# Loading the hi parts of streamed weights with a second, casting DMA on GpSimd's queue instead of copying them on ScalarE

## The chip, the cores and the metric

One NeuronCore of a Trainium2 chip runs the whole program. The metric is the device time of one execution in microseconds, lower is better. The kernel before was timed in three runs: 1090.1, 1091.72 and 1093.24 us, so the median is 1091.72 us.

## The reference

The reference is a two-layer decoder trunk in float32: 512 tokens, 1024 channels. Each layer normalises x (RMSNorm with a gain), multiplies it by a wide input projection, and feeds three mixers with slices of the result: a causal differential attention (4 heads of 2 x 64 dims, rotary), a gated convolution of width 3, and a chunkwise retention (4 heads). Each mixer's output is gated, projected to 1024 channels by its own matrix, weighted by a sigmoid gate, and the sum goes through an output projection back into x. A last RMSNorm closes it. Cut to what matters here:

```python
def hybrid_layer(x, norm_g, w_in, ..., w_branch, w_out, layer):
    h = rms_norm(x, norm_g)
    proj = h @ w_in
    (aq, ak, av, az, cx, cb, cc, cz, rq, rk, rv, rz, gates) = jnp.split(proj, split_points, axis=-1)
    a = diff_attention(aq, ak, av, ...) * silu(az)
    c = short_conv(cx, cb, cc, conv_w) * silu(cz)
    r = retention(rq, rk, rv) * silu(rz)
    merged = sum(sigmoid(gates[i]) * (branch[i] @ w_branch[i]) for i in range(3))
    return x + merged @ w_out
```

## The kernel before, in words

**Products in parts.** TensorE multiplies in the type fp32r, which keeps fewer bits than float32. So every float32 operand is split into a hi part (the value rounded to fp32r) and a lo part (the value minus its hi part), and `mm3` (L186 to L189) adds three products: hi by hi (L187), hi of the weight by lo of the activation (L188), lo of the weight by hi of the activation (L189). The split of a tile is a copy by ScalarE that rounds (L183) and a subtraction (L180), done by VectorE or GpSimd.

**The weight stream.** The weights of both layers are laid out as 184 chunks of 128 partitions x 1024 float32 (512 KB), in the order of use (`chunk_order`). A chunk feeds 24 products of TensorE (8 blocks of K, three products each). `prefetch` (L196) issues the load of a chunk into a buffer `wraw` on SyncE's queue; there are three such buffers. `split_next` (L203) takes the oldest loaded chunk and makes its parts `whi` and `wlo`, three buffers each. It works on two halves of 512 columns: ScalarE copies each half into `whi`; VectorE subtracts for the first half and GpSimd for the second. `chunk` (L214) hands the next parts to the caller and keeps one more chunk split ahead (LOOK = 1).

**The order of work.** TensorE's order is the program's (a manual schedule for that engine). The other engines' orders come from the framework's scheduler, which also places all semaphores: a load into `wraw` waits until both subtractions of the chunk three earlier have read it, a copy into `whi` until TensorE's products L187 and L188 of the chunk three earlier have read it, and a subtraction into `wlo` likewise for L189. Every engine runs its own queue strictly in order, so an instruction that waits holds up all that is queued behind it.

**The start.** SyncE issues, one after the other, half of chunk 0, the first tile of x, the other half of chunk 0, then the other seven tiles of x with chunks 1 and 2 between them (L257 to L266). ScalarE makes the hi parts of x times the gain (L349) and squares (L309, one buffer `sq`), GpSimd adds the squares up (L315), and after three chunks of products TensorE sums them over the channels (L323), before the fourth chunk.

**The end.** The output projection of layer 2 runs twice over its 8 chunks, once per half of the tokens (`out_proj`, L661; the loop at L697). Its products are only 256 columns wide, so a chunk is used up in half the time, and GpSimd also adds squares there (L315, 128x256).

Of the kernel before, what the change touches and what calls it, by code (L numbers as in the profile page):

```python
# [18 lines left out]
P = 128  # L19
# [10 lines left out]

# Column offsets of the input projection.
AQ, AK, AV, AZ = 0, 512, 1024, 1536
# [3 lines left out]

# Columns of the small-parameter array.
PG, PCONV, PSUB, PFIN, PW = 0, 16, 40, 42, 50


# [1 line left out]
def merge_chunks(br, jp):  # L42
# [12 lines left out]
def chunk_order(layer):  # L55
    """Chunks of a layer: ("B", col, c) is 512 columns of w_in with K blocks 2c and
    2c+1; ("A", col) 128 columns with all of K; ("W", br, c) 256 columns of
    w_branch; ("O", c) 128 columns of w_out."""
    L = [("B", c, i) for c in (AV, RV) for i in range(4)]
    L += pair_chunks(AK, AQ, AZ)  # L60
    for i in range(4):
        L += conv_chunks(i)
    L += pair_chunks(AK + 256, AQ + 256, AZ + 256)
    for jp in range(4):
        L += merge_chunks(1, jp)
    L += pair_chunks(RK, RQ)
    for jp in range(4):
        L += [("A", RZ + P * jp)] + merge_chunks(0, jp)
    for jp in range(4):
        L += merge_chunks(2, jp)  # L70
    for _ in range(1 if layer < DEPTH - 1 else 2):
        L += [("O", c) for c in range(8)]
    return L


def rot_perm(base):
    """Column order of a rotation head pair block: the two halves of a pair lie
    16 partitions apart within a block of 32."""
    idx = []
    for h in range(4):  # L80
        for ihi in range(2):
            for half in range(2):
                for ilo in range(16):
                    idx.append(base + h * 64 + half * 32 + ihi * 16 + ilo)
    return idx
# [32 lines left out]
def tables():  # L118
    """Rotation tables (attention, then retention k and q of each head pair, the
    decays folded in) and the constant matrices."""  # L120
    f = np.float32
    pos = np.arange(S, dtype=f)
    inv = (f(500000.0) ** (-np.arange(0, 16, 2, dtype=f) / f(16))).astype(f)
    ang = (pos[:, None] * inv[None, :]).astype(f).astype(np.float64)
    tab = np.zeros((5, P, 2, S))
    tab[0, :, 0] = 1.0
    for p in range(P):
        d = p % 64
        if d < 16:
            tab[0, p, 0] = np.cos(ang[:, d % 8])  # L130
            tab[0, p, 1] = np.sin(ang[:, d % 8]) * (-1.0 if d < 8 else 1.0)
    inv = (f(1.0) / (f(10000.0) ** np.linspace(0.0, 1.0, 32, dtype=f))).astype(f)
    ang = (pos[:, None] * inv[None, :]).astype(f).astype(np.float64)
    pd = np.arange(S, dtype=np.float64)
    for blk in range(2):
        for p in range(P):
            h = 2 * blk + p // 64
            r = p % 64
            i = (r // 32) * 16 + r % 16
            sg = -1.0 if (r // 16) % 2 == 0 else 1.0  # L140
            lg = math.log(1.0 - 2.0 ** (-5 - h))
            c, s = np.cos(ang[:, i]), sg * np.sin(ang[:, i])
            gk, gq = np.exp(-pd * lg) * 0.125, np.exp(pd * lg)
            tab[1 + 2 * blk, p] = c * gk, s * gk
            tab[2 + 2 * blk, p] = c * gq, s * gq
    cm = np.zeros((P, 4, P))
    cm[:, 0] = np.eye(P)
    cm[:, 1] = np.triu(np.full((P, P), NEG), 1)
    cm[:, 2] = np.triu(np.ones((P, P)))
    cm[:, 3] = 1.0 / P  # L150
    return tab.reshape(5, P, 2 * S).astype(f), cm.reshape(P, 4 * P).astype(f)
# [3 lines left out]
def tile_hybrid_trunk(ctx: ExitStack, tc: tile.TileContext, xT, w, prm, lam, tab, cmat, outT):  # L155
# [34 lines left out]

# [1 line left out]
    order = [(l, c) for l in range(DEPTH) for c in chunk_order(l)]  # L192
# [3 lines left out]
    def prefetch():  # L196
        i = pos[0] + len(parts) + len(raws)
        if i < len(order):
            raw = t("wraw", 3, (P, 1024))
            nc.sync.dma_start(raw, w[i])  # L200
            raws.append(raw)

    def split_next():  # L203
        if not raws:
            prefetch()
        if raws:
            raw = raws.pop(0)
            hi, lo = tr("whi", 3, (P, 1024)), tr("wlo", 3, (P, 1024))
            for c in range(0, 1024, 512):
                c = slice(c, c + 512)  # L210
                split(hi[:, c], lo[:, c], raw[:, c], G if c.start else V)
            parts.append((hi, lo))

    def chunk(l, *key):  # L214
        """Next chunk in parts; the one after it is on its way."""
        assert order[pos[0]] == (l, key), (order[pos[0]], l, key)
        while len(parts) < min(LOOK + 1, len(order) - pos[0]):
            split_next()
        pos[0] += 1
        return parts.pop(0)  # L220

# [1 line left out]
    # Projections are cut into ticks of 12 products. The steps of the attentions,  # L223
    # whose products wait for other engines, are placed between them: each part of
    # a step comes a few ticks after the one it depends on.
    now = [0]
# [14 lines left out]

# [1 line left out]
    par = t("par", 1, (P, PW))  # L243
    nc.sync.dma_start(par, prm)
    eps = t("eps", 1, (P, 1))
    G.memset(eps, EPS)
    # The tensor engine comes up to its clock, and the scalar engine's functions
    # load, while the first tiles arrive.
    warm = t("wb", 1, (P, S), mybir.dt.bfloat16)
# [5 lines left out]
    x = []  # L255
    raw = t("wraw", 3, (P, 1024))
    nc.sync.dma_start(raw[:, 0:512], w[0, :, 0:512])  # L257
    for k in range(NK):
# [3 lines left out]
        if k == 0:  # L262
            nc.sync.dma_start(raw[:, 512:], w[0, :, 512:])
            raws.append(raw)
        elif k % 2 == 0 and len(raws) < 3:
            prefetch()  # L266
# [6 lines left out]
    G.memset(ones_d, 1.0 / D)  # L273
    # -lambda of each layer on every partition, and the sub-norm gains.
    nlam, gsub = [], []
# [23 lines left out]
    class Rms:  # L299
        """Statistics of the tiles of x over their channels, for tokens q0 to q1."""  # L300

# [3 lines left out]
        def add(self, xk, end=False):  # L305
            """A tile; the end tile's squares stay apart, for a short way to the sums."""
            n = self.n
# [9 lines left out]
        def column(self):  # L317
            """1/rms as a column of each token tile."""
            nt = self.n // P
# [11 lines left out]
        def row(self, col):  # L331
            """1/rms as a row on every partition, in PSUM."""
            row = pa()
# [5 lines left out]
    for l in range(DEPTH):  # L339
        last = l == DEPTH - 1  # L340
        ng = [par[:, PG + 8 * l + k:PG + 8 * l + k + 1] for k in range(NK)]

# [1 line left out]
        xg = {}  # L344
# [8 lines left out]

# [1 line left out]
        def values(col, banks, cs):  # L355
# [34 lines left out]

# [1 line left out]
        h = []  # L392
# [26 lines left out]

        # Queries and keys of two heads (or components) of 64 dims, stacked on the  # L420
        # partitions so that one product carries hi*hi + lo*hi; the third part
        # multiplies the query's hi rows with the key's lo rows.
        H = [slice(0, 64), slice(64, 128)]
# [23 lines left out]
        def mm_qk(outs, a, asl, b, bsl):  # L447
            """Two of them; their half-height parts lie in different rows of the array."""
            for i in range(2):
# [7 lines left out]

        # sigmoid(v) = (1 + tanh(v/2)) / 2, which needs no other table than Exp's; the
        # halves are left to later steps.
        def tanh_half(out, o):  # L460
# [11 lines left out]
        def head_out(o, z, g, out):  # L472
            """Normalised, gated head output in parts; o is [v dim, token], z twice the
            gate and g a factor that takes it back."""
            sq = t("sq", 1)
# [19 lines left out]

# [1 line left out]
        rbr, rz = [], {}  # L497
# [19 lines left out]

# [1 line left out]
        cbr = []  # L519
# [18 lines left out]

# [1 line left out]
        abr, az = [], {}  # L540
# [7 lines left out]
        def attn_step(hd, i, o, wt, qk):  # L548
            """Scores and weights of one query tile; every second one, the values."""
            q, k = qk[hd]  # L550
# [50 lines left out]

# [1 line left out]
        m = [None] * NK  # L603
# [48 lines left out]

# [1 line left out]
        x2 = []  # L654
# [6 lines left out]
        def out_proj(q0, q1):  # L661
            """The tiles of the output in turn; the last parts of m come late, so that
            the first two tiles' products with them wait behind the others."""
            ws, os = {}, {}
# [70 lines left out]
```

## Time and profile before

| what | value |
|---|---|
| median of 3 runs | 1091.72 us (1090.1 to 1093.24) |
| span of the profiled execution, first to last instruction | 1090.5 us |
| the profiled execution's own time | not given; its span lies 1.2 us under the median |
| TensorE products busy | 1078.6 us, 99% of the span |
| ScalarE, VectorE, GpSimd busy | 504.6, 676.4, 329.8 us |
| mean granted TensorE clock | 0.996 of full speed |
| moved by DMA | 113.64 MB, 104 GB/s in the mean |

How to read it: a busy share is an average over stages with different limits, and TensorE's matmuls are pipelined with modelled ends, so 99% busy says that it hardly ever waited, not that it ran at its peak. PE is TensorE's products and PEld its weight loads, ACT is ScalarE, DVE VectorE, POOL GpSimd, SP SyncE; SPq is SyncE's queue. L180 and L183 are lines of helpers, so the tile's name (whi, wlo, st, xb) tells which use is meant. A few per cent of the matmul records may be missing.

### The profile page before, as it was taken

What the parts mean: (1) busy time and instruction counts of PE and PEld (TensorE: products, weight loads), DVE (VectorE), ACT (ScalarE), POOL (GpSimd) and SP (SyncE); (2) the same over time, 40 slices, a digit from 0 to 9 for tenths busy, and PEclk for the clock granted to TensorE, in tenths of its full rate; (3) what the DMA queues carried; (4) which work ended last, traced back from release to release, by engine and by line L of the source; (5) the groups of instructions that cost most, each with busy time, mean ns of one, the idle gap of its engine ahead of it and who ended that gap; (6) DMA issues with size and microseconds to landing.
All of it is one profiled execution on the core that took longest, in us unless ns stands there. A gap on an engine that the chain in (4) does not pass through costs nothing.

```text
span 1090.5 us, 13839 instructions
## 1 busy us (share of the span) xinstructions
PE 1078.6 (99%) x5010; PEld 878.1 (81%) x5010; DVE 676.4 (62%) x1158; ACT 504.6 (46%) x944; POOL 329.8 (30%) x258
## 2 busy tenths in 40 slices
PE   8999999999999999999999999999999999999997
PEld 6888888888887778888888878888788877788896
DVE  6787686755676556444438766868546946654344
ACT  6454453543554445333444535445344635543343
POOL 6222223221232232323532212232123223232264
PEclk9999999999999999999999999999999999999999
DMA  6322222232234122434422232223212322124353
GB/s 232 117 96 97 78 77 82 94 116 79 77 116 136 58 78 78 135 129 129 158 87 97 86 109 78 78 82 124 85 59 97 135 97 73 62 97 132 111 197 123
DMA packets 34340, 113.64 MB, mean 104 GB/s; under 512 B 3936, under 2 KB 3936, under 8 KB 34272
## 3 DMA queue, kind: packets, MB, share of 16 engines
q1 hardware_dynamic: 34272, 112.76, 30.2%
q8 instruction: 39, 0.64, 0.2%
q14 instruction: 29, 0.24, 0.1%
HBM read 108.55 MB, written 4.19 MB: 103 GB/s over the span
## 4 chain that ended last, share of the span: by engine, by line
PE 97%; POOL 1%; DMA 1%; ACT 0%; DVE 0%; issue 0%; SPq 0%; DVEq 0%; POOLq 0%; ACTq 0%
PE pj L187 29%; PE pj L189 28%; PE pj L188 28%; PE pa L451 3%; PE pa L187 3%; PE pa L188 2%; PE pa L189 2%; PE pa L577 1%; POOL e L315 1%; DMA wraw<-w 1%; PE pa L485 0%; PE pa L484 0%; POOL wlo L180 0%; DVE p L693 0%; PE pa L323 0%
## 5 line engine op out<-in xcount | busy, mean ns | idle before, releaser
L180 POOL TENSOR_TENSOR wlo<-wraw,whi 128x512 fp32r<-128x512 f32 x184 | 252.6, 1375 | 640.4 <-ACT whi L183 619.0
L187 PE MATMUL pj<-h,whi 128*128 128x512 f32 x960 | 384.6, 401 | 0.0
L188 PE MATMUL pj<-h,whi 128*128 128x512 f32 x960 | 375.9, 392 | 0.0
L189 PE MATMUL pj<-h,wlo 128*128 128x512 f32 x960 | 375.7, 391 | 0.0
L183 ACT CAST whi<-wraw 128x512 fp32r<-128x512 f32 x368 | 217.1, 617 | 241.3 <-PE pj L188 178.9
L180 DVE TENSOR_TENSOR wlo<-wraw,whi 128x512 fp32r<-128x512 f32 x184 | 152.9, 832 | 131.7 <-ACT whi L183 128.3
L189 PEld LDWEIGHTS pj<-h,wlo 128*128 128x128 f32 x960 | 180.2, 188 | 41.3
L187 PEld LDWEIGHTS pj<-h,whi 128*128 128x128 f32 x960 | 180.4, 188 | 40.5 <-issue 1.7
L188 PEld LDWEIGHTS pj<-h,whi 128*128 128x128 f32 x960 | 180.6, 188 | 35.2
L187 PE MATMUL pj<-xb,whi 128*128 128x512 f32 x192 | 76.3, 397 | 0.0
L189 PE MATMUL pj<-xb,wlo 128*128 128x512 f32 x192 | 75.3, 392 | 0.0
L188 PE MATMUL pj<-xb,whi 128*128 128x512 f32 x192 | 75.0, 390 | 0.0
L564 ACT ACTIVATE p<-pa,nm 128x128 f32<-128x128 f32 (+3 forms) x64 | 33.4, 525 | 70.5 <-DVE nm L561 70.0
L488 DVE RECIPROCAL e<-e 128x512 f32<-128x512 f32 x16 | 53.6, 3351 | 18.1 <-ACT e L487 18.1
L183 ACT CAST st<-pa 128x256 fp32r<-128x256 f32 (+2 forms) x80 | 29.7, 372 | 74.7 <-DVE pa L506 43.1
L187 PE MATMUL pj<-vm,whi 128*128 128x256 f32 (+1 forms) x192 | 61.0, 318 | 0.0
L189 PE MATMUL pj<-vm,wlo 128*128 128x256 f32 (+1 forms) x192 | 60.7, 316 | 0.0
L188 PE MATMUL pj<-vm,whi 128*128 128x256 f32 (+1 forms) x192 | 60.6, 316 | 0.0
L621 DVE SCALAR_TENSOR_TENSOR wb<-wa,pj 128x512 f32<-128x512 f32 x32 | 22.0, 688 | 44.9 <-PE pj L189 44.9
L451 PE MATMUL pa<-qk 128*128 128x256 f32 (+3 forms) x192 | 46.5, 360 | 0.0
L451 PEld LDWEIGHTS pa<-qk 128*128 128x128 f32 x192 | 29.8, 185 | 19.1 <-issue 13.6
L180 DVE TENSOR_TENSOR st<-pa,st 128x256 fp32r<-128x256 f32 (+2 forms) x80 | 33.7, 421 | 18.4 <-ACT st L183 18.2
(123 smaller groups left out, 1414.7 us busy)
## 6 DMA issues: line engine op xcount, KB each, us to landing
wraw<-w SPq DMA_DIRECT2D x183, 512.0 KB, 3.3
tab<-tab SPq DMA_DIRECT2D x10, 512.0 KB, 3.3
xm<-xT SPq DMA_DIRECT2D x16, 256.0 KB, 3.5
xsave<-xm SPq DMA_DIRECT2D x8, 256.0 KB, 2.0
xm<-xsave SPq DMA_DIRECT2D x8, 256.0 KB, 2.7
outT<-p SPq DMA_DIRECT2D x8, 256.0 KB, 2.1
wraw<-w SPq DMA_DIRECT2D x2, 256.0 KB, 3.1
cm<-cmat SPq DMA_DIRECT2D x1, 256.0 KB, 6.6
```

Of the source, the lines that this page charges most:

```text
L180: eng.tensor_tensor(lo, x, hi, op=ALU.subtract)
L183: A.copy(hi, x)
L187: T.matmul(out, wh, xh, start=start, stop=False)
L188: T.matmul(out, wh, xl, start=False, stop=False)
L189: T.matmul(out, wl, xh, start=False, stop=stop)
L315: G.tensor_tensor(self.acc[:, :n], self.acc[:, :n], sq[:, :n], op=ALU.add)
L451: T.matmul(o, ac[i][:, asl], bc[i][:, bsl], start=i == 0, stop=i == 1)
L488: V.reciprocal(r, r)
L564: A.activation(pc[:, :n], sp[:, :n], AF.Exp, bias=nm, scale=0.125, accum_out=sm)
L577: T.transpose(tp[:, j * P:(j + 1) * P], p1[:, j * P:(j + 1) * P], ident)
L621: V.scalar_tensor_tensor(y, g, 1.0, o, op0=ALU.add, op1=ALU.mult)
```

## The change

`prefetch` now issues two loads of each chunk: the plain one on SyncE's queue into `wraw` as before, and a second one of the same 512 KB on GpSimd's queue into `whi`, whose type is fp32r, so that the DMA does the rounding. `whi` gets four buffers instead of three. ScalarE's copies go, for all chunks but chunk 0, which is loaded in two halves and still copied. The subtractions stay where they were (VectorE for the first half, GpSimd for the second), and now wait for both loads. Comments were removed as well.

```diff
     def prefetch():
         i = pos[0] + len(parts) + len(raws)
         if i < len(order):
-            raw = t("wraw", 3, (P, 1024))
+            raw, hi = t("wraw", 3, (P, 1024)), tr("whi", 4, (P, 1024))
             nc.sync.dma_start(raw, w[i])
-            raws.append(raw)
+            nc.gpsimd.dma_start(hi, w[i])
+            raws.append((raw, hi))

     def split_next():
         if not raws:
             prefetch()
         if raws:
-            raw = raws.pop(0)
-            hi, lo = tr("whi", 3, (P, 1024)), tr("wlo", 3, (P, 1024))
+            raw, hi = raws.pop(0)
+            loaded = hi is not None
+            if not loaded:
+                hi = tr("whi", 4, (P, 1024))
+            lo = tr("wlo", 3, (P, 1024))
             for c in range(0, 1024, 512):
                 c = slice(c, c + 512)
-                split(hi[:, c], lo[:, c], raw[:, c], G if c.start else V)
+                if not loaded:
+                    A.copy(hi[:, c], raw[:, c])
+                lo_part(lo[:, c], raw[:, c], hi[:, c], G if c.start else V)
             parts.append((hi, lo))
...
         if k == 0:
             nc.sync.dma_start(raw[:, 512:], w[0, :, 512:])
-            raws.append(raw)
+            raws.append((raw, None))
```

## Rows read from the trace of the kernel before

**Rows 1.** Page, part 1: busy time, share of the span, instructions of an engine.

```profile
PE 1078.6 (99%) x5010; PEld 878.1 (81%) x5010; DVE 676.4 (62%) x1158; ACT 504.6 (46%) x944; POOL 329.8 (30%) x258
```

**Rows 2.** Page, part 4: the chain that ended last, by engine.

```profile
PE 97%; POOL 1%; DMA 1%; ACT 0%; DVE 0%; issue 0%; SPq 0%; DVEq 0%; POOLq 0%; ACTq 0%
```

**Rows 3.** Waits of TensorE: who waited for whom, total us, times, longest.

```profile
PE pa L323 <- POOL e L315: 2.5, 1, 2.5
...
PEld pj L187 <- ACT whi L183: 1.3, 7, 0.2
PEld pa L187 <- ACT whi L183: 1.0, 4, 0.2
```

**Rows 4.** Page, part 5: groups that split the weights; busy, mean ns, idle before.

```profile
L180 POOL TENSOR_TENSOR wlo<-wraw,whi 128x512 fp32r<-128x512 f32 x184 | 252.6, 1375 | 640.4 <-ACT whi L183 619.0
...
L183 ACT CAST whi<-wraw 128x512 fp32r<-128x512 f32 x368 | 217.1, 617 | 241.3 <-PE pj L188 178.9
L180 DVE TENSOR_TENSOR wlo<-wraw,whi 128x512 fp32r<-128x512 f32 x184 | 152.9, 832 | 131.7 <-ACT whi L183 128.3
```

**Rows 5.** Windows: stretch, length, PE PEld DVE ACT POOL busy (instructions), PE clock, DMA, GB/s.

```profile
10.00:15.00 5.00, 5.00 (x24) 4.14 (x23) 4.36 (x4) 3.33 (x7) 3.66 (x3) 1.00 1.05 405
...
25.00:30.00 5.00, 4.52 (x18) 3.76 (x19) 4.55 (x6) 3.81 (x8) 4.44 (x4) 0.73 0.33 108
...
50.00:88.00 38.00, 38.00 (x168) 31.22 (x167) 31.76 (x44) 19.70 (x33) 7.96 (x6) 1.00 0.29 97
...
320.00:337.00 17.00, 17.00 (x76) 13.96 (x75) 16.72 (x22) 10.41 (x17) 4.28 (x3) 1.00 0.51 167
...
1041.00:1060.50 19.50, 19.50 (x168) 19.50 (x167) 9.85 (x16) 11.26 (x24) 15.46 (x14) 1.00 0.60 201
1063.00:1082.00 19.00, 18.32 (x161) 18.23 (x159) 10.21 (x22) 9.98 (x20) 12.48 (x11) 1.00 0.35 124
```

**Rows 6.** Timeline of the start: ScalarE, GpSimd and TensorE.

```profile
9.38 1.14 ACT L183 CAST whi<-wraw 128x512 fp32r<-128x512 f32 x2 [0.56 <-DMA wraw<-w]
...
10.60 1.62 POOL L180 TENSOR_TENSOR wlo<-wraw,whi 128x512 fp32r<-128x512 f32 x1 [0.69 <-ACT whi L183]
...
14.66 1.29 POOL L315 TENSOR_TENSOR e<-e,sq 128x512 f32<-128x512 f32 x1 [0.74 <-ACT sq L309]
...
24.15 1.28 POOL L315 TENSOR_TENSOR e<-e,sq 128x512 f32<-128x512 f32 x1 [0.74 <-ACT sq L309]
...
25.48 1.05 PE L323 MATMUL pa<-ones_d,e 128*128 128x1 f32 x8 [2.51 <-POOL e L315]
26.39 0.48 PE L187 MATMUL pj<-whi,xb 128*128 128x512 f32 x1
...
30.82 0.39 PE L187 MATMUL pj<-whi,xb 128*128 128x512 f32 x1
```

**Rows 7.** Timeline of ScalarE: start us, us, what; two copies each in mid-kernel, two at the end.

```profile
523.10 1.14 ACT L183 CAST whi<-wraw 128x512 fp32r<-128x512 f32 x2 [3.16 <-PE pj L188]
...
528.59 1.14 ACT L183 CAST whi<-wraw 128x512 fp32r<-128x512 f32 x2 [3.21 <-PE pj L188]
...
1046.96 1.14 ACT L183 CAST whi<-wraw 128x512 fp32r<-128x512 f32 x2 [1.32 <-PE pj L188]
...
1058.27 1.14 ACT L183 CAST whi<-wraw 128x512 fp32r<-128x512 f32 x2 [1.37 <-PE pj L188]
```

**Rows 8.** DMA issues of the page, and one issue on SyncE's timeline.

```profile
wraw<-w SPq DMA_DIRECT2D x183, 512.0 KB, 3.3
...
3.54 0.43 SPq L200 DMA_DIRECT2D wraw<-w  x1
```

**Rows 9.** The tile wlo: duration ns min/median/max of its subtractions, first and last start.

```profile
L180 DVE TENSOR_TENSOR wlo<-wraw,whi x184: 628/693/1799, 4.6 to 1074.5; 128x512 fp32r<-128x512 f32 x184
L180 POOL TENSOR_TENSOR wlo<-wraw,whi x184: 1277/1297/2197, 6.9 to 1074.2; 128x512 fp32r<-128x512 f32 x184
```

## The prediction, made before the changed kernel ran

> **What bounds the kernel now.** I read the busy shares first: TensorE is busy for 1078.6 of 1090.5 us and ScalarE for 504.6 [rows 1]. The chain that ended last says the same from the other side, 97% of it is TensorE [rows 2]. So the third view is TensorE's list of waits, to see what of the rest could be won: one wait of 2.5 us for GpSimd's sum of squares at the start, and 1.3 + 1.0 us in 11 pieces for ScalarE's copies into `whi` [rows 3]. The reader should see that the work that is removed, 217.1 us of copies [rows 4], is almost nowhere on TensorE's path. The long waits that the copies cause, 619.0 us on GpSimd and 128.3 us on VectorE [rows 4], are idle time of engines that have it to spare: a chunk's parts are made about two chunks ahead of their use.
>
> Two stretches are tighter than that average, and the windows show them. At the start the DMA engines are full (share 1.05 at 405 GB/s from 10 to 15 us) [rows 5], and GpSimd's adds end only when TensorE already waits [rows 6]. At the end a chunk lasts 1058.27 - 1046.96 = 11.31 us for 4, or 2.83 us, against 5.49 us in mid-kernel [rows 7]; there GpSimd is busy for 15.46 of 19.5 us and DMA has a share of 0.60 [rows 5].
>
> **The copies that go.** 366 of 368 copies of 617 ns, 226 us of ScalarE's time at that mean (217.1 us for all when overlaps count once) [rows 4]. What of it lies on the path is bounded by the two waits above, 0 to 2.3 us [rows 3]. They are 0.2 us each at the longest and sit where a product needs several things at once, so I take 0.
>
> **The loads that come: mid-kernel.** 183 loads of 512 KB on GpSimd's queue. A plain load lands 3.3 us after its issue [rows 8]. With four `whi` buffers the load of a chunk may start when TensorE is done with the chunk four earlier, three chunk times, 3 x 5.49 = 16.5 us, before its first use [rows 7]. Issue, landing and subtraction (about 1, 3.3 and 1.4 us) need some 6 us of it. The wait for TensorE's release, 178.9 us on ScalarE's queue before [rows 4], moves to GpSimd's queue. Behind it there stand the subtractions of `wlo`, of the heads' `st` and `xb`, and the adds of squares; the same queue already waited 619 us for copies without TensorE waiting for it, so I cost the move at 0. The cover is the two chunks of lead; without it each chunk would pay up to the landing time. DMA traffic goes from about 97 GB/s to about twice that [rows 5], half of what the start reached. SyncE's queue gains nothing to issue, but its loads share the DMA engines.
>
> **The price of one issue on GpSimd.** No row shows one. Below, the nearest row is an issue on SyncE's queue, 0.43 us [rows 8]; above, one GpSimd instruction over such a half tile, 1.375 us [rows 4]. They are close enough together to take the middle, 0.9 us. In mid-kernel this is 0.9 us in 5.49 on an engine with 70% idle, hidden.
>
> The Trainium skill, DMA: Bandwidth & Descriptors, section Latency and other measured facts, gives about 1 us to the first byte for a load from GpSimd against 0.6 us from SyncE; if all of that 1 us held the queue, the terms below would grow by 0.1 us per issue, to a sum some 1 us longer; no row here shows that latency.
>
> **The start.** Two things are added. (a) Bytes: the casting loads of chunks 1 to 3 need no buffer to come free and can be issued at once, 3 x 0.524 MB, 3.9 us of DMA at 405 GB/s [rows 5], mixed with the first tiles of x and with chunk 1. Chunk 1 landed at 9.38 us, and GpSimd's half of its lo part was done at 12.22 [rows 6]; the copy that now falls out gives back 1.1 us. Bounds 0 to 3.9 us; I take 1, nearer the low end, because the loads are spread over tiles that have a microsecond or two of slack. (b) Issues: those of chunks 4 to 6 wait for chunks 0 to 2 and can fall between the adds that TensorE waits for. GpSimd has idle pieces of 0.74 us there, four of them, since each add waits for a square [rows 6]. Bounds 0 (all in those pieces or behind the last add) to 3 x 1.375 = 4.1 us; I take 3 x 0.9 = 2.7 less half, 1.3 us. TensorE waits there already, so each microsecond of it counts in full. What it loses to the clock is paid before: after its 2.5 us wait the granted clock is 0.73 from 25 to 30 us [rows 5], that is, between its 1.2 and 2.4 GHz levels.
>
> **The end.** From 1041 to 1060.5 us seven chunks pass. GpSimd: 15.46 + 7 x 0.9 = 21.8 us in 19.5, 2.3 us too much [rows 5]. In the second pass few loads are left and 12.48 of 19 us grow by 3 or 4 issues, which fits. DMA: 0.60 of full for 201 GB/s becomes about 1.16, 3.0 us over in that window, if a casting load costs what a plain one does. These two lie beside each other, and a lead of one to two chunks (2.83 us each [rows 7]) goes against them. I take 2 us. Bounds: 0, and with 1.375 us per issue 15.46 + 9.6 - 19.5 = 5.6 us.
>
> **Sum.** 0 + 1 + 1.3 + 2 = 4.3 us on the profiled span of 1090.5 is 1094.8. The median of the runs lies 1.2 us above that span, so 1096.0 us, 0.4% slower.
>
> **The rivals.** No change: the scheduler places the issues behind the adds at the start, and the lead covers the end; both terms fall to about 0, and the time is 1091.7. For it speaks that TensorE waits for almost nothing in 1090 us [rows 3]; against it that the start has no slack at all on GpSimd.
>
> Faster: with ScalarE free, squares and hi parts of x come sooner and GpSimd's adds end before 22.97 us (25.48 - 2.51), when TensorE begins to wait [rows 6]. That wins the 2.5 us and the slow clock behind it: 26.39 to 30.82 us is 4.4 us for the 12 products there, at the usual spacing of 5.49 / 24 = 0.23 us 2.7, so 1.7 us. 1091.7 - 4.2 = 1087.5. It decides only if the last add moves by 2.5 us. Against it: the adds waited 0.74 us each for a square that itself waited for the single buffer, not for copies.
>
> DMA as the bound: a casting load runs at half the plain rate. Then the window of the end needs 0.60 + 2 x 0.60 = 1.8 times its length, 15.6 us over, less some 5 of lead, and the start pays its 3.9 us or more: about 1091.7 + 15 = 1107. No row shows a casting load, for or against.
>
> VectorE as the bound: today the copies of the two halves end 0.57 us apart (1.14 for two [rows 7]), so VectorE's subtraction (median 693 ns) is nearly done when GpSimd's (1297) starts. With one load for both they start together, and the longest rows, 1799 and 2197 ns [rows 9], show what one waiting for the other would make of it. If VectorE lost 1.1 us (1799 - 693) per chunk, the stretch 320 to 337 us, where it is busy for 16.72 of 17, would grow by about 3 x 1.1 - 0.3 = 3.0 us, and 50 to 88 us (31.76 of 38) by 7 x 1.1 - 6.2 = 1.5 us [rows 5]; twice each for two layers, 9 us, on top of the forecast about 1105. The Trainium skill, SBUF — State Buffer, section Who interferes with whom, has this rule: a VectorE instruction with two SBUF inputs and a GpSimd instruction that reads SBUF shut each other out. The spread of the durations [rows 9] agrees with it, without showing that it is the cause.
>
> That the load rounds nothing is possible as well; the lo parts would then be zero, and the time as forecast.
>
> **How the numbers follow.** About 0.3%, 3.3 us, is what a measurement of this kernel can tell from no change. Forecast 0.35 (1093.5 to 1099), no change 0.34, faster 0.12, DMA bound 0.11, VectorE bound 0.08. A sliver of the forecast, 0.04, lies within 0.3%: so faster 0.12, same 0.38, slower 0.50. The range leaves out most of the faster case and the upper half of the DMA case, 0.16 together: 1088.5 to 1107.
>
> **What would show it.** In the profile after: ScalarE near 504.6 - 217 = 288 us; a second DMA queue with 96 MB; `wlo` waiting for DMA instead of ScalarE; TensorE's L323 waiting 3 to 5 us instead of 2.5; a few short waits of TensorE after 1041 us, for `wlo` or `whi`; none between 40 and 1030 us. The forecast is wrong if L323 waits less than before, if TensorE waits in mid-kernel, or if subtractions on VectorE lengthen beyond a mean of 1.1 us.

## The result, and the profile after

The changed kernel takes 1143.2 us (median of 4 runs, 1139.2 to 1144.3) against 1091.9 us for the kernel before on the same chip. The measured ratio is 1.0457, 95% interval 1.0440 to 1.0475 (the two medians by themselves give 1.0470). It is slower, as forecast, but by 51 us where 4.3 were forecast, and far outside the range.

The page of the changed kernel: busy time of the engines, two DMA queues, three groups that split the weights, and two DMA issues with their KB and us to landing.

```profile
PE 1105.9 (97%) x5010; PEld 886.2 (78%) x5010; DVE 707.0 (62%) x1158; ACT 308.9 (27%) x578; POOL 436.4 (38%) x441
...
q1 hardware_dynamic: 34272, 112.76, 30.6%
q0 software_dynamic: 26352, 95.96, 26.8%
...
L180 POOL TENSOR_TENSOR wlo<-wraw,whi 128x512 fp32r<-128x512 f32 x184 | 259.2, 1409 | 128.4 <-DMA whi<-w 70.6
L180 DVE TENSOR_TENSOR wlo<-wraw,whi 128x512 fp32r<-128x512 f32 x184 | 175.1, 951 | 192.7 <-PE pj L189 94.0
L201 POOL DMA_DIRECT2D whi<-w x183 | 104.1, 569 | 463.7 <-issue 268.5
...
whi<-w POOLq DMA_DIRECT2D x183, 512.0 KB, 4.4
wraw<-w SPq DMA_DIRECT2D x183, 512.0 KB, 4.2
```

The change did what it says: ScalarE lost 196 us of work against [rows 1], a second queue moves 96 MB, and GpSimd's subtraction waits for a load instead of a copy [rows 4]. One issue holds GpSimd for 0.569 us. A plain load now lands in 4.2 us instead of 3.3 [rows 8]. Per megabyte the two queues take the same DMA time (26.8 / 95.96 = 0.279 and 30.6 / 112.76 = 0.271 per cent), so a casting load costs the DMA engines no more than a plain one. No engine became the bound. What is new is in TensorE's list of waits (who waited for whom; us in total, times, longest):

```profile
PE pa L329 <- POOL e L321: 8.5, 2, 7.0
PE pj L189 <- DVE wlo L180: 7.4, 7, 1.8
PE pj L187 <- ACT h L183: 6.1, 3, 3.0
PE pj L187 <- DMA whi<-w: 2.7, 2, 1.5
PE pj L187 <- ACT xb L355: 2.0, 1, 2.0
```

Before, the first of these was 2.5 us and the others were not there [rows 3]. They sum to 27 us, half of what is lost, so the waits alone don't tell it. A part of the rest is TensorE's clock behind a wait. The windows of the changed kernel around its wait of 3.0 us, which ends at 73.5 us (length; busy time and instructions of TensorE, its weight loads, VectorE, ScalarE, GpSimd; granted clock, DMA share, GB/s):

```profile
70.00:75.00 5.00, 2.01 (x6) 1.04 (x5) 3.92 (x5) 2.20 (x4) 2.26 (x2) 0.84 0.28 91
75.00:80.00 5.00, 5.00 (x19) 3.96 (x19) 3.86 (x8) 0.74 (x2) 2.02 (x2) 0.81 0.32 120
```

From 73.5 to 76.8 us the granted clock is 0.50, the lower of its two levels, and products then start 0.43 us apart instead of 0.23.

I therefore paired TensorE's instructions of the two traces one by one and took the difference of their start times. The table gives this delay in us at seven products, for one profiled execution of the changed kernel and of each experiment told below (the head line is the product's start in the kernel before):

```
product at          26.4   60.4   94.0  582.6  638.4 1039.6 1083.7
changed kernel       8.8    9.7   19.0   24.7   36.7   40.8   51.6
e1_ahead             9.4   10.2   10.7   16.4   17.3   21.4   29.8
e2_three             6.0    6.7    7.2   86.2   87.0  155.7  173.8
e3_vector            7.6    9.4    9.9   15.6   16.4   20.5   24.4
e4_plain            -0.6   -0.1   -0.1    6.0    6.0    6.0    6.0
e6_mid               0.1    0.1    0.1    3.8    3.8    6.0    6.3
e8_place            -0.1    0.6    1.1    6.8    7.6   11.7   12.5
e9_late              9.0    9.7   10.1   14.6   15.2   18.1   28.5
e10_align           -0.1   -1.7   -1.7   -1.7   -1.7   -1.7   -1.4
e11_ahead_late       8.6    8.4    8.4   12.1   12.1   14.2   24.4
e11_after_late       9.0   10.3   17.2   20.8   31.3   35.0   44.5
```

The first line falls into four losses. **The start**: 9.7 us by 60 us. **The tiles of h**: 9.3 us from 60 to 94 us, and 12.0 us where layer 2 begins (582 to 638). **A slow growth** where TensorE waits for nothing: 5.7 us over layer 1 and 4.1 over layer 2, some 2.4 ns for every product. **The end**: 10.8 us. By kind, the 51.6 us are 24.5 of longer waits, 11 of products under the lower clock behind them, and a rest of 16 that is mostly the growth (12.5 us over the whole kernel where it stands alone, in e8).

For the second loss, GpSimd's timeline of the changed kernel, as layer 1 gets going and as layer 2 does (start, duration, what; in brackets the idle time ahead of it and what ended it):

```profile
33.35 1.75 POOL L180 TENSOR_TENSOR wlo<-wraw,whi 128x512 fp32r<-128x512 f32 x1
35.03 0.57 POOL L201 DMA_DIRECT2D whi<-w  x1
40.70 1.80 POOL L180 TENSOR_TENSOR wlo<-wraw,whi 128x512 fp32r<-128x512 f32 x1 [5.10 <-DMA whi<-w]
42.46 0.57 POOL L201 DMA_DIRECT2D whi<-w  x1
48.25 1.81 POOL L180 TENSOR_TENSOR wlo<-wraw,whi 128x512 fp32r<-128x512 f32 x1 [5.22 <-DMA whi<-w]
...
583.20 1.80 POOL L180 TENSOR_TENSOR wlo<-wraw,whi 128x512 fp32r<-128x512 f32 x1 [5.22 <-DMA whi<-w]
584.95 0.58 POOL L201 DMA_DIRECT2D whi<-w  x1
590.66 1.80 POOL L180 TENSOR_TENSOR wlo<-wraw,whi 128x512 fp32r<-128x512 f32 x1 [5.14 <-DMA whi<-w]
```

This is a circle. The subtraction waits for a load that was issued just ahead of it, and the next issue stands behind the subtraction in the same queue. One load is in flight at a time, and four buffers don't help. A turn costs the issue, the landing and the subtraction: 48.25 - 40.70 = 7.55 us, where TensorE uses up a chunk in 5.49 [rows 7]. VectorE's half of the subtraction then waits too, ahead of its work on `h`. VectorE's timeline of the changed kernel, five waits for the load and one instruction on the way to `h`:

```profile
48.20 0.69 DVE L180 TENSOR_TENSOR wlo<-wraw,whi 128x512 fp32r<-128x512 f32 x1 [3.22 <-DMA whi<-w]
...
55.64 0.69 DVE L180 TENSOR_TENSOR wlo<-wraw,whi 128x512 fp32r<-128x512 f32 x1 [1.49 <-DMA whi<-w]
...
62.96 0.69 DVE L180 TENSOR_TENSOR wlo<-wraw,whi 128x512 fp32r<-128x512 f32 x1 [0.60 <-DMA whi<-w]
...
70.40 0.69 DVE L180 TENSOR_TENSOR wlo<-wraw,whi 128x512 fp32r<-128x512 f32 x1 [0.72 <-DMA whi<-w]
71.01 1.75 DVE L401 SCALAR_TENSOR_TENSOR wa<-xm,par,e 128x512 f32<-128x512 f32 x1
...
77.92 0.69 DVE L180 TENSOR_TENSOR wlo<-wraw,whi 128x512 fp32r<-128x512 f32 x1 [1.14 <-DMA whi<-w]
```

They come every 7.3 to 7.5 us, at GpSimd's pace. Up to 70.40 us VectorE has lost 3.22 + 1.49 + 0.60 + 0.72 = 6.0 us in them, and TensorE's wait of 3.0 us for `h`, which ends at 73.5 us, falls between two of them. Only 17 chunks have this order in GpSimd's queue: 8 near the start of each layer and the last one. Elsewhere the scheduler put one further load ahead of the subtraction.

For the start, GpSimd's timeline of the changed kernel again:

```profile
12.60 1.30 POOL L180 TENSOR_TENSOR wlo<-wraw,whi 128x512 fp32r<-128x512 f32 x1 [1.76 <-DMA wraw<-w]
15.23 1.65 POOL L180 TENSOR_TENSOR wlo<-wraw,whi 128x512 fp32r<-128x512 f32 x1 [1.32 <-DMA wraw<-w]
16.84 1.74 POOL L321 TENSOR_TENSOR e<-e,sq 128x512 f32<-128x512 f32 x1
...
32.13 1.26 POOL L321 TENSOR_TENSOR e<-e,sq 128x512 f32<-128x512 f32 x1 [0.74 <-ACT sq L315]
```

Three subtractions now stand ahead of the adds of squares, two of them waiting for raw loads that land late. The last add begins at 32.13 us where it began at 24.15 [rows 6], 8.0 us later. The subtractions are not most of it: in e3_vector below GpSimd makes none, and its last add still begins 6.8 us late. ScalarE and GpSimd in e3_vector:

```profile
16.46 1.41 ACT L355 ACTIVATE xb<-xm,par 128x512 fp32r<-128x512 f32 x2 [1.28 <-DMA xm<-xT]
...
18.48 1.64 POOL L321 TENSOR_TENSOR e<-e,sq 128x512 f32<-128x512 f32 x1 [1.69 <-ACT sq L315]
...
30.92 1.26 POOL L321 TENSOR_TENSOR e<-e,sq 128x512 f32<-128x512 f32 x1 [0.74 <-ACT sq L315]
```

The adds wait for squares, and on ScalarE's queue the next square stands behind hi parts of x that wait for tiles of x landing late. How much each of the two paths carries in the changed kernel was not tested.

### The profile page after: what moved, and what is told of

Read it like the earlier page. It is cut to its first block, busy times and chain, and to the rows that moved or that the text cites. A ratio compares the mean times of both kernels' runs of the same rounds, so it can differ in the third digit from the quotient of the medians.

```text
span 1142.4 us, 13653 instructions
## 1 busy us (share of the span) xinstructions
PE 1105.9 (97%) x5010; PEld 886.2 (78%) x5010; DVE 707.0 (62%) x1158; ACT 308.9 (27%) x578; POOL 436.4 (38%) x441
## 3 DMA queue, kind: packets, MB, share of 16 engines
q1 hardware_dynamic: 34272, 112.76, 30.6%
q0 software_dynamic: 26352, 95.96, 26.8%
## 5 line engine op out<-in xcount | busy, mean ns | idle before, releaser
L187 PE MATMUL pj<-h,whi 128*128 128x512 f32 x960 | 390.0, 406 | 6.7 <-ACT h L183 6.1
L189 PE MATMUL pj<-h,wlo 128*128 128x512 f32 x960 | 382.8, 399 | 4.5 <-DVE wlo L180 4.5
L188 PE MATMUL pj<-h,whi 128*128 128x512 f32 x960 | 380.9, 397 | 0.2 <-DVE h L180 0.2
L180 POOL TENSOR_TENSOR wlo<-wraw,whi 128x512 fp32r<-128x512 f32 x184 | 259.2, 1409 | 128.4 <-DMA whi<-w 70.6
L180 DVE TENSOR_TENSOR wlo<-wraw,whi 128x512 fp32r<-128x512 f32 x184 | 175.1, 951 | 192.7 <-PE pj L189 94.0
L201 POOL DMA_DIRECT2D whi<-w x183 | 104.1, 569 | 463.7 <-issue 268.5
L187 PE MATMUL pj<-vm,whi 128*128 128x256 f32 (+1 forms) x192 | 62.5, 325 | 2.7 <-DMA whi<-w 2.7
L188 PE MATMUL pj<-vm,whi 128*128 128x256 f32 (+1 forms) x192 | 61.7, 321 | 0.3 <-DVE vm L180 0.3
L467 ACT ACTIVATE wa<-pj 128x512 f32<-128x512 f32 x48 | 28.7, 599 | 100.0 <-PE pj L189 98.1
```

What stands on the lines that cost most here:

```text
L180: eng.tensor_tensor(lo, x, hi, op=ALU.subtract)
L187: T.matmul(out, wh, xh, start=start, stop=False)
L188: T.matmul(out, wh, xl, start=False, stop=False)
L189: T.matmul(out, wl, xh, start=False, stop=stop)
L201: nc.gpsimd.dma_start(hi, w[i])
L467: A.activation(out, o, AF.Tanh, scale=0.5)
```

## The experiments

No kernel leaves out any part of the computation; e4, e5 and e7 add loads that nothing uses. The first theory was that the order in GpSimd's queue makes the loss at `h`. Its rivals were the extra DMA traffic, the casting itself, and collisions of VectorE with GpSimd.

**e1_ahead: the order in the queue.** Both loads are asked for one chunk earlier, and GpSimd's subtraction is held behind the next issue.

```
-        if not raws:
+        for _ in range(2 - len(raws)):
             prefetch()
...
-                lo_part(lo[:, c], raw[:, c], hi[:, c], G if c.start else V)
+                if c.start and loaded:
+                    with tc.issue_after(issued[-1].ins):
+                        lo_part(lo[:, c], raw[:, c], hi[:, c], G)
+                else:
+                    lo_part(lo[:, c], raw[:, c], hi[:, c], G if c.start else V)
```

> Edit: each casting load is issued one chunk earlier in the program, and GpSimd's subtraction of a chunk is put behind the casting load of the next chunk on GpSimd's queue. In the changed kernel this order already holds for most chunks, but not for the 17 chunks 3 to 10 and their like in layer 2, whose subtraction stands ahead of the next load. Theory (queue order: with the load behind the subtraction only one casting load is in flight, and a chunk costs issue 0.57 + landing 5.1 + subtraction 1.8 = 7.5 us against 5.5 us of products): the waits at h in both layers go, some 12 us in layer 2 and some 8 in layer 1, so 1118 to 1128 us. Rival (the doubled bytes make every load late, whatever the order): within 5 us of 1143. Rival (VectorE and GpSimd shut each other out in the subtractions): within 5 us of 1143, since both still start together.

Measured: 1124.7 us, ratio 1.0294 (1.0271 to 1.0318). GpSimd's timeline in this kernel, and one instruction of VectorE's:

```profile
43.63 0.57 POOL L201 DMA_DIRECT2D whi<-w  x1 [3.74 <-PE pa L189]
44.22 1.30 POOL L180 TENSOR_TENSOR wlo<-wraw,whi 128x512 fp32r<-128x512 f32 x1
50.00 0.58 POOL L201 DMA_DIRECT2D whi<-w  x1 [4.47 <-issue]
...
55.97 2.05 DVE L180 TENSOR_TENSOR h<-wa,h 128x512 fp32r<-128x512 f32 x1 [0.69 <-ACT h L183]
```

The issue comes first, the subtraction follows without a wait, and issues are paced by TensorE. In the table the steps at `h` shrink from 9.3 to 0.5 us and from 12.0 to 0.9, some 20 us in all. VectorE is still held up there while GpSimd subtracts (2.05 us for a subtraction of `h` that otherwise takes 0.69), so such collisions alone don't make the loss. The edit also parts the two loads of a chunk, which matters, as e2 shows. The start, the growth and the end stay.

**e2_three: three buffers instead of four**, nothing else.

> Edit: three whi buffers instead of four. The scheduler then puts the subtraction ahead of the next casting load for 146 chunks instead of 17. Theory (queue order): about 1 to 2 us lost for each of the 129 more, so 1250 to 1400 us, with a period of the loads near 7.5 us through most of the kernel. Rival (doubled bytes): the same bytes, so 1135 to 1155 us. Rival (VectorE and GpSimd collide): 1135 to 1155 us as well.

Measured: 1266.2 us (one run), within the expectation. Here 146 chunks have the bad order in the queue. TensorE waits 41.8 us in 20 pieces for `whi` itself and 22.8 in 21 for VectorE's part, and its mean clock drops to 0.946. But the table shows no step at the tiles of `h` (0.5 and 0.8 us), although the order is bad there too. GpSimd's timeline of e2_three in that stretch of layer 1:

```profile
50.56 1.28 POOL L180 TENSOR_TENSOR wlo<-wraw,whi 128x512 fp32r<-128x512 f32 x1 [3.48 <-DMA whi<-w]
...
56.00 1.28 POOL L180 TENSOR_TENSOR wlo<-wraw,whi 128x512 fp32r<-128x512 f32 x1 [3.35 <-DMA whi<-w]
```

The casting loads from 40 to 70 us with their KB and us to landing, in the changed kernel and in e2_three, and SyncE's plain load in the changed kernel at 42.5 us:

```profile
whi<-w POOLq DMA_DIRECT2D x4, 512.0 KB, 5.5
```

```profile
whi<-w POOLq DMA_DIRECT2D x6, 512.0 KB, 3.9
```

```profile
42.53 0.33 SPq L200 DMA_DIRECT2D wraw<-w  x1
```

A turn takes 5.44 us here, about a chunk's time, and nothing is lost. In the changed kernel both loads of a chunk are issued 0.07 us apart (42.46 and 42.53) and share the DMA engines; the casting one lands in 5.5 us, and the subtraction lasts 1.8. In e2 the plain load follows 0.7 to 3.1 us later, the casting one lands in 3.9 us, and the subtraction lasts 1.28. So the bad order by itself makes a turn of one load at a time, and it costs time where that turn is longer than a chunk. No run parts the two loads and does nothing else. Around 600 us a turn of e2 takes 7.2 us, and its losses lie in such stretches.

**e3_vector: both halves of the subtraction on VectorE**, so that nothing in GpSimd's queue waits for a load.

```
-                lo_part(lo[:, c], raw[:, c], hi[:, c], G if c.start else V)
+                lo_part(lo[:, c], raw[:, c], hi[:, c])
```

> Edit: VectorE does both halves of the subtraction, so that no wait for a landing stands on GpSimd's queue ahead of a casting load, and no subtraction of the stream collides between the two engines. Theory (queue order): the loads run as early as their buffers allow; VectorE gets 184 x 0.69 = 127 us more work and bounds the stretches where it was full (h, rotations), so a gain of some 10 us in the start and the boundary of the layers against some loss there: 1115 to 1140 us. Rival (doubled bytes): 1143 or above. Rival (collisions): well below, 1100 to 1115 us, since the collisions are gone.

Measured: 1115.7 us, ratio 1.0212 (1.0194 to 1.0230). The steps at `h` are 0.5 and 0.8 us, as in e1, with another edit: a wait for the landing ahead of the next issue is what the two remove in common. GpSimd now makes no subtraction of weights at all, and the growth is still there, so collisions of these two are not its cause. The end costs 3.9 us instead of 10.8: GpSimd's subtractions carry about two thirds of that loss.

**e4_plain: the kernel before with unused plain loads** of layer 1's weights on SyncE's queue.

```
+            if order[i][0] == 0:
+                nc.sync.dma_start(t("wdum", 1, (P, 1024)), w[i])
```

> Edit: the kernel before, plus a second, plain load of each chunk of layer 1 into one buffer that nothing reads, on SyncE's queue; ScalarE still makes the hi parts. It adds the bytes alone, in layer 1 alone. Theory (queue order): products of layer 1 take 2 to 3 ns longer each, about 5 us, and the start loses 2 to 4 us; layer 2 as in the kernel before; 1096 to 1101 us. Rival (doubled bytes are the cause): layer 1 loses half of the 51 us, 1112 us or more.

Measured: 1098.3 us (ten runs, 1093.6 to 1101.4), ratio 1.0052 (1.0033 to 1.0070), with no growth between the products. The time is as expected and the reason is not: it is one stall of 6 us, where TensorE waits twice for VectorE in the rotation of queries and keys, the stretch in which VectorE had no slack before (16.72 of 17 us [rows 5]). TensorE's timeline in this kernel:

```profile
333.25 0.47 PE L187 MATMUL pj<-h,whi 128*128 128x512 f32 x1 [1.41 <-DVE wa L417]
...
336.53 0.50 PE L189 MATMUL pj<-h,wlo 128*128 128x512 f32 x1 [2.56 <-DVE wlo L180]
```

What delays VectorE there was not followed up. Twice the bytes by themselves do not slow TensorE's products.

**e5_cast and e7_pool: the kernel before with unused loads of layer 1 on GpSimd's queue**, casting and plain.

```
+            if order[i][0] == 0:
+                nc.gpsimd.dma_start(tr("wdum", 1, (P, 1024)), w[i])
```

(e7_pool has `t` for `tr`, so that nothing is cast.)

> Edit: the kernel before, plus a second load of each chunk of layer 1 into one fp32r buffer that nothing reads, on GpSimd's queue, with the cast. Theory (the growth per product comes from casting loads on GpSimd's queue, since the plain bytes on SyncE's queue gave none): products of layer 1 take 2 to 3 ns longer each between the waits, products of layer 2 do not; in all 1096 to 1115 us, the waits of GpSimd for its one buffer included. Rival (it comes from TensorE waiting on a DMA's semaphore instead of ScalarE's): no growth, since nothing waits for these loads.

> Edit: as e5_cast, but the unused buffer is plain float32, so the load on GpSimd's queue casts nothing. If the growth of 2 to 3 ns per product in layer 1 is there as in e5_cast, it belongs to loads issued from GpSimd; if it is gone, to the cast. I expect the former. Time within 5 us of e5_cast.

Measured: 1180.4 and 1178.0 us, one run each. That e7 lies within 5 us of e5 was expected; that they lie 88 and 85 us above the kernel before was not. The waits of e5_cast:

```profile
POOL wdum L202 <- DMA wdum<-w: 198.7, 66, 4.7
...
PE pa L487 <- POOL st L180: 39.7, 4, 16.5
```

The unused tile has one buffer, so each issue waits for the landing of the one before, and GpSimd's whole queue stands behind it: 198.7 us in 66 waits. It is the fault of the change in a purer form. For the growth the two runs answer what they were made for: between the waits the delay stands still in both, so it comes neither from the cast nor from issuing on GpSimd.

**e6_mid: e1 with the start and the end as before.** The first 12 and the last 18 chunks are copied by ScalarE; 154 casting loads remain.

```
-            raw, hi = t("wraw", 3, (P, 1024)), tr("whi", 4, (P, 1024))
+            raw, hi = t("wraw", 3, (P, 1024)), None
...
+            if 12 <= i < len(order) - 18:
+                hi = tr("whi", 4, (P, 1024))
+                issued.append(nc.gpsimd.dma_start(hi, w[i]))
```

> Edit: the kernel with the loads one chunk ahead (e1_ahead), and chunks 0 to 11 and the last 18 copied by ScalarE as in the kernel before; 154 of 184 chunks have the casting load. Theory: no loss at the start (first product at 5.9 us, TensorE's wait for the sum of squares near 2.5 us) and none at the end; what is left is the slow growth of 2 to 3 ns per product while casting loads run, some 9 us in all: 1098 to 1105 us. Rival (the losses at start and end come from the new order of the queues, not from the casting loads there): 1110 us or more.

Measured: 1098.9 us, ratio 1.0055 (1.0039 to 1.0072). The start costs 0.1 us and the end 0.3, so both losses belong to the casting loads of those chunks. The growth, expected to stay, is gone as well. What is left is one stall in each layer, 3.7 and 2.1 us; 1.6 us of the first are the lower clock behind it. The first of them on the timelines of this kernel (VectorE, GpSimd, TensorE), and the same chunk's subtraction on VectorE in the changed kernel:

```profile
224.96 2.13 DVE L180 TENSOR_TENSOR wlo<-wraw,whi 128x512 fp32r<-128x512 f32 x1
225.26 1.27 POOL L180 TENSOR_TENSOR wlo<-wraw,whi 128x512 fp32r<-128x512 f32 x1
...
227.15 0.50 PE L189 MATMUL pj<-h,wlo 128*128 128x512 f32 x1 [1.81 <-DVE wlo L180]
```

```profile
242.80 0.69 DVE L180 TENSOR_TENSOR wlo<-wraw,whi 128x512 fp32r<-128x512 f32 x1
```

VectorE's subtraction, 0.69 us as a rule [rows 9], lasts 2.13 while GpSimd's 1.27 lie inside it, and TensorE waits for it. In the changed kernel the same subtraction lies clear of GpSimd's, lasts 0.69, and TensorE doesn't wait. The Trainium skill, SBUF — State Buffer, section Who interferes with whom, says that such a pair shut each other out; these rows agree with it (0.69 + 1.27 = 1.96), and no run here takes one of the two away at this place alone.

**The growth: e8 to e11.** The kernels that grow and those that don't differed in one more thing, which no source line of the diff shows: the memory address of `whi`. The changed kernel names `whi` in the prefetch at the head, so it is allocated ahead of the parts of x (`xb`), at byte 32,160 of a partition; in the kernel before and in e6 it lies behind them at 69,696. The difference of 37,536 bytes is the size of the tiles named between (`xb` 32,768, `wa` 2,048, `cm` 2,048, `ones_p` 512, and five small ones at 32 each). In e4, e5 and e7 the unused tile of 4,096 bytes comes on top, which leaves the place within 256 bytes as it was. Five kernels move it, and do nothing else but give it the fourth buffer in e8 and e10. e8 names the tile early in the kernel before, with four buffers and no load or copy changed:

```
     raw = t("wraw", 3, (P, 1024))
+    t("xm", 8)
+    tr("whi", 4, (P, 1024))
```

> The kernel before with the float32r buffers of the hi parts given the memory address that they have in the changed kernel (32,160 per partition, ahead of the tiles of x; in the kernel before 69,696, behind them), by naming the tile earlier, and four of them for three; no load and no copy is changed. Placement theory of the slow growth (2.5 ns per product in every kernel with the low address, none in those with the high one): the growth is there without a single casting load, about 4,300 products by 2.5 ns = 10 us, so about 1102 us, 1099 to 1105. Rival (the growth comes from the casting loads of the first twelve chunks or from what their lateness shifts): no growth, 1091 to 1094 us.

Measured: 1104.9 us, ratio 1.0114 (1.0099 to 1.0129), without a single casting load. Its delay in the table runs like the changed kernel's between the steps. e9 goes the other way, naming the other tiles first in e1:

> The kernel with the loads asked one chunk ahead of GpSimd's subtraction (1124.7 us), with the hi buffers at the high address (69,568) and nothing else changed. Placement theory: the growth of 2.5 ns per product is gone, the losses at the start and the end stay, 1124.7 - 10 = 1115 us, 1111 to 1118. Rival: the growth stays as it was, 1123 to 1127 us.

Measured: 1121.6 us, ratio 1.0270 (1.0252 to 1.0288): neither theory's number. The growth fell from 2.4 to 1.8 ns per product and no further, at 69,568, which is 128 bytes short of 69,696. So not the position but the offset of the address was left, and e10 tests it: e8 with an unused tile of 672 bytes ahead of `whi` (and 96 behind it).

```
     t("xm", 8)
+    t("pad0", 1, (P, 168))
     tr("whi", 4, (P, 1024))
+    t("pad1", 1, (P, 24))
```

> The kernel before with four hi buffers ahead of the tiles of x, as in the run that showed the growth without a load, but 672 bytes further (32,832 for 32,160), by an unused tile ahead of them: so they begin at the same offset in 256 bytes as in the kernel before (64), where they began at 160. If the offset in 256 bytes sets the growth: none, 1091 to 1095 us. If it is the low position as such: the growth of 2.5 ns per product stays, 1102 to 1106 us.

Measured: 1092.5 us, ratio 1.0007 (0.9997 to 1.0016). The windows from 100 to 500 us, of the kernel before, of e8 and of e10 (length; busy time and instructions of TensorE, its weight loads, VectorE, ScalarE, GpSimd; granted clock, DMA share, GB/s):

```profile
100.00:500.00 400.00, 400.00 (x1802) 321.97 (x1801) 247.89 (x442) 182.94 (x348) 107.61 (x83) 1.00 0.28 95
```

```profile
100.00:500.00 400.00, 400.00 (x1784) 318.91 (x1783) 242.96 (x445) 181.91 (x345) 117.62 (x83) 1.00 0.29 95
```

```profile
100.00:500.00 400.00, 400.00 (x1801) 321.99 (x1801) 243.73 (x438) 182.84 (x346) 118.80 (x85) 1.00 0.29 95
```

All three show TensorE busy throughout at the full clock, at the same DMA traffic; only the number of products tells that e8 is slower, by 18 in 1802, or 1%. A busy share of 100% hides it. The last two runs put `whi` at 69,696 in e1 and in the changed kernel itself:

```
     raw = t("wraw", 3, (P, 1024))
+    t("xm", 8)
+    t("cm", 1, (P, 4 * P))
+    tr("ones_p", 1, (P, P))
+    t("ones_d", 1, (P, 1))
+    t("wa", 1)
+    for tag in ("nlam0", "gsub0", "nlam1", "gsub1"):
+        t(tag, 1, (P, 1))
+    tr("xb", 16)
```

> The kernel with the loads asked one chunk ahead of GpSimd's subtraction (1124.7 us), with all tiles named in the order of the kernel before, so that the hi buffers begin at 69,696 as there. Placement theory: no growth left (2.5 ns per product before, 1.8 at 69,568), the losses at the start and the end stay: 1124.7 - 10 to 12 = 1113 to 1115 us, 1110 to 1117. Rival (the casting loads cause a part of the growth of their own): 1119 to 1125 us.

> The changed kernel with nothing but the hi buffers moved to 69,696, the address of the kernel before. Placement theory: 1143.2 - 10 to 12 = 1131 to 1133 us, 1128 to 1136, with the losses of the start, of the waits for h at both layer starts and of the end left. Rival (no effect of the place on the changed kernel): 1140 to 1145 us.

Measured: 1119.5 us, ratio 1.0247 (1.0230 to 1.0264), and 1135.2 us, ratio 1.0394 (1.0376 to 1.0411). The growth is gone in both (0.2 ns per product or less). The times fell by less than 10 us because the stalls of e6 appeared, 3.7 and 2.1 us in the one and 3.6 and 3.7 in the other; the growth seems to have kept the two subtractions apart. In e1 the gain was 5.2 us instead of 10 to 12, and by its time alone that run lies in the rival's range (1119 to 1125). It is the delay between the stalls that decides: it stands still in both kernels, with all casting loads in them. So the placement theory holds for the growth in the changed kernel, and no part of it is left for the casting loads.

No version with casting loads beats the kernel before; e6, with fewest, is 0.55% slower.

## Why the prediction was wrong

**Mid-kernel: the step that failed.** "I cost the move at 0", with "the two chunks of lead" as its cover. I checked the wait for TensorE's release, which moves to GpSimd's queue, and what stands behind it. I did not check the other wait on that queue, that of the subtraction for the landing, against the issue that stands behind it. Where the queue has the two in this order one load is in flight at a time, whatever the number of buffers: 7.55 us per chunk instead of 5.49. The turn itself was mis-sized too: "some 6 us", from a landing of 3.3 us, a load's time when it is alone, where this one lands in 5.5 beside the plain load issued with it. And the lead was smaller than two chunks: in the kernel before, a chunk's parts are ready some 8 us (median) ahead of the first product that uses them, 1.4 chunk times, and in the changed kernel this falls from 8.0 us at chunk 4 to 0.6 at chunk 8. The prediction even had the price, "without it each chunk would pay up to the landing time", and took the cover for granted. e1 and e3 remove the order and with it some 20 of the 51.6 us.

**A term that was missing: some 10 us of growth.** Neither the sum nor a rival held that moving a tile's first use moves its address, and that TensorE's products notice. e8, e10 and e11 show it.

**The start, mis-sized.** Forecast +2.3 us, measured 9.7. The extra bytes were the right place and I took the low end of their bounds (1 of 0 to 3.9 us). Three casting loads are issued ahead of most tiles of x, and what I missed is what waits for these: ScalarE's hi parts of x, with squares behind them in its queue, and GpSimd's subtractions ahead of the adds. The last add slipped by 8.0 us and TensorE's wait went from 2.5 to 7.0, with the first product 1.7 us late. "What it loses to the clock is paid before" failed too: behind TensorE's wait of 2.0 us for its first operands the granted clock is 0.80 from 10 to 15 us, where it was 1.00 [rows 5], and from 30 to 35 us it is 0.50; products under the lower clock are some 2.5 of the 9.7 us. The windows of the changed kernel:

```profile
10.00:15.00 5.00, 5.00 (x19) 3.96 (x18) 3.10 (x4) 3.26 (x5) 2.15 (x2) 0.80 1.04 413
...
30.00:35.00 5.00, 1.56 (x8) 1.56 (x8) 0.69 (x1) 1.96 (x3) 4.13 (x3) 0.50 0.66 253
```

With two such loads at the head instead of three (e2) the first product behind the sums is 6.0 us late instead of 8.8. The issues cost little: 0.569 us each, inside the bounds and under the 0.9 taken, and only one stands among the adds. e6 takes the first loads away, and the whole term goes.

**The end, mis-sized.** Forecast 2 us, bounds 0 to 5.6, measured 10.8. The place and the engine were right: e3 frees GpSimd of its subtractions and pays 3.9. The windows of the changed kernel, for the seven chunks that took 19.5 us before [rows 5]:

```profile
1081.80:1107.50 25.70, 22.44 (x172) 21.72 (x171) 10.65 (x14) 2.93 (x7) 18.14 (x20) 0.93 0.87 277
```

They take 25.7 us, and GpSimd is busy in 18.14 of them, not all: the rest it waits, for landings and for its turn. I had added busy times as if an engine that waits in order could fill its gaps. The estimate of the DMA engines' work was close: 0.87 of 25.7 us, where 1.16 of 19.5 was forecast.

**The rivals.** No change: refuted by 51 us. DMA as the bound: refuted; the casting loads cost the DMA engines what plain ones do, and e4 bears the bytes. The bytes count through the landing time, in the circle and at the start. VectorE as the bound: not the cause of the loss at `h` or of the growth, as e1, e3 and e11 show (its subtractions went from a mean of 0.832 to 0.951 us, not beyond 1.1); a small part of it is real, the stalls of 2 to 4 us in e6 and e11, and 1.75 us for an L401 while GpSimd subtracts. Faster: TensorE's first wait grew instead of shrinking. Rounding: ScalarE's copies were replaced, and the time doesn't bear on it.

**What held.** Slower was the likeliest sign. ScalarE's copies were off the path: 196 us of them gone won nothing. The second queue's 96 MB were right; ScalarE's busy time came out at 308.9 and not 288: the copies' records overlap with those of their neighbours (two copies of [rows 6] end at 10.52 us, and ScalarE's next instruction begins at 10.43), so a group's busy time can't be taken off the engine's; all other instructions of ScalarE cover 309.2 us in the trace before. And the prediction named its own test: wrong "if TensorE waits in mid-kernel", which it does.

## What to carry to other kernels

When a load's issue moves to an engine that also computes with what was loaded, read the order of that engine's queue: an instruction that waits for the landing should not stand ahead of the next issue, or one load is in flight whatever the buffers. Then compare the turn (issue, landing beside whatever is issued with it, work) with the time of a chunk: here 7.55 us lost time and 5.44 did not. Count the lead in issues that stand ahead of the wait. Count behind each wait of TensorE also what the lower clock costs. And when a tile is named earlier than before, compare its address with the old one before blaming the edit for a loss that no wait shows.

## What the runs showed that I had not expected

The address of `whi` changes the rate of TensorE's products by 1% at an unchanged granted clock. With `whi` at 69,696 or at 32,832, both 64 bytes past a multiple of 256, there is no growth; at 32,160 (160 past) it is 2.4 ns for a product of some 229, at 69,568 (192 past) 1.8. In the products with `h`, where `whi` is the operand loaded as weights, the largest part lies in the step from a product with `wlo` to the next one with `whi` (5.2 ns in e8, 6.5 in e9; 2.6 or less in the other two steps). Which property of the address counts stays open: four addresses don't give the rule, and in e9 the tiles of `xb` moved by 128 bytes too. Nor is it shown why the scheduler gave 17 chunks, and 146 with three buffers, the bad order.
